# Projecting two value groups together, with 512 moving columns

## The chip, the cores and the metric

The kernel runs on one core of a Trainium2 chip. The metric is device time in microseconds, the median of several executions. Of each kernel one execution is also recorded by the hardware profiler; its times are counted from the first instruction. The core's engines are TensorE (PE, matmuls, with PEld for the loads of the stationary operand), VectorE (DVE), ScalarE (ACT), GpSimd (POOL) and SyncE (SP), whose queue issues nearly all DMA transfers. Each engine works through its own instructions in order and waits for others by semaphores.

## The reference

Two layers over a sequence of 512 tokens of width 1024. In each layer one projection of the residual stream feeds two mixers of eight heads of width 64 and an indexer:

```python
proj = jnp.einsum('bsd,dn->bsn', x, w_in)
qA, kA, vA, gA, qB, kB, vB, gB, qI, kI, wI = jnp.split(proj, SPLIT_POINTS, axis=-1)
oA = stick_breaking_attention(heads(qA, HEADS_A), heads(kA, HEADS_A), heads(vA, HEADS_A))
oB = dsa_sparse_attention(heads(qB, HEADS_B), heads(kB, HEADS_B), heads(vB, HEADS_B),
                          qI.reshape(b, s_len, IDX_HEADS, IDX_DIM), kI, wI, rel_bias, topk)
mix = jnp.concatenate([oA * jax.nn.silu(gA), oB * jax.nn.silu(gB)], axis=-1)
y = jnp.einsum('bsm,md->bsd', mix, w_out)
return layer_norm(ALPHA * x + y, ln_g, ln_b)
```

Mixer A is stick-breaking attention: with z the scaled scores, a key's weight is sigmoid(z) times the product of (1 - sigmoid(z)) over the keys between it and the query. Mixer B takes, for each query, the 128 keys that the indexer scores highest, and does a soft-max with a bias by relative position over them. The gate silu(g) is g times sigmoid(g).

## The kernel before

All products are made in three matmuls: each fp32 operand is split into a high part and a low rest (`hi`, `lo`), and high times high, low times high and high times low are summed in PSUM. The residual stream lies transposed in `XH` and `XL` as 4 token blocks by 8 chunks of 128 channels. `XN` holds it in its natural order; between the start of a layer and slot 59 that tile is free.

The projection is cut into units of 256 columns, named by group, half and kind: `("A", 1, "v")` is the values of the second four stick heads, `("B", 0, "v")` those of the first four soft-max heads. For queries, keys and gates (`project_t`, L274) the weights are stationary and 512 tokens move, one chunk of 128 columns after the other. For values (`project_v`, L286) the tokens are stationary and the 256 weight columns move, one token block after the other. Each unit's weights are two tiles of 1024 elements per partition. The class `Stream` loads them (two raw buffers, L193), splits them (ACT makes the high part, L212, POOL the low part, L215) into four buffers, and keeps about two tiles ahead (`prep_ahead`, at the end of each slot).

A layer is a loop over slots (L899), one attention task per slot: slots 0 to 23 are the indexer, 24 to 39 the four heads of A0, 40 to 55 those of A1, 56 to 71 those of B0, 72 to 87 those of B1; a task is one block of 128 queries of one head, with 128 to 512 keys. The order of all engines' work is written out by hand in this loop. Of a task, PE makes the scores in its slot (`product`, L518 and L523, into two PSUM buffers). A stick task then has a Sigmoid on ACT (L717), a scan on DVE a slot later (L722), and PE transposes the result three slots after the scores (L530). A soft-max task has a sum with the bias and a minimum on DVE (L762; the bias and mask are added on POOL a slot before, L753), an Exp on ACT (L767) and its transposes two slots after the scores. The transposed weights are copied by ACT (L727, L538) and their low parts made by DVE (L730, L541), and when a head is complete PE multiplies them with its values (L701) and the output is mixed: a copy on ACT (L600), a sum on DVE (L602) and, where the gate is there already, a product on POOL (L603). In some slots DVE stores bias plus mask of later heads in `XN` (L980).

The projection units fill PE between these steps. `fills` (L75) gives their order, each with a pin: the slot by which it is to be done. `fill` (L836) is called up to three times a slot and runs as many steps as the line between the pins asks for, counting 648 for three 512-wide matmuls and 324 for three 256-wide ones. What a unit leaves in PSUM is evacuated at the next `flush`, early in the following slot. The pins that matter:

```python
units += [("A", 1, "g"), ("A", 1, "k"), ("A", 1, "q"), ("A", 1, "v")]
units += [("A", 0, "g"), ("B", 0, "g"), ("B", 1, "g"), ("B", 0, "k"), ("B", 0, "q")]
units += [("B", 0, "v"), ("B", 1, "k"), ("B", 1, "q"), ("B", 1, "v")]
A_PINS = (29, 32.5, 36, 40, 44, 47.4, 50.6, 53.8, 56.8)
B_PINS = (62.5, 67, 71, 79)
```

So the values of A1 are made from slot 36 to 40 and those of B0 from 56.8 to 62.5; the gates are done by 29, 44, 47.4 and 50.6. A query chunk is evacuated by two ACT and two DVE instructions, a key chunk by the same and two DMA copies (`evac_q`, `evac_k`), a gate chunk by a Sigmoid on ACT and a product on DVE, and one more product on POOL if the head's output is there (`gate`, L582). B0's value blocks go from PSUM to their tile `vt` by ACT and DVE (`evac_v`, L355). A1's are first copied to `V_NOW`, in the tile `M`; three DMA copies shift them by one token into `V_PREV` (`shift_values`, L322), and two slots later DVE takes the difference and ACT and DVE split it (`value_steps`, L335). The tiles `vt` come from a pool of two.

Of the kernel before, what the change touches and what calls it, by code (L numbers as in the profile page):

```python
# [17 lines left out]
P = 128  # L18
# [39 lines left out]
A_PINS = (29, 32.5, 36, 40, 44, 47.4, 50.6, 53.8, 56.8)  # L58
# [12 lines left out]
HALF_SLOTS = 5  # L71
B_PINS = (62.5, 67, 71, 79)


def fills():  # L75

    units = [("I", 1, "q"), ("A", 0, "k"), ("A", 0, "q")]
    units += [("A", 1, "g"), ("A", 1, "k"), ("A", 1, "q"), ("A", 1, "v")]
    units += [("A", 0, "g"), ("B", 0, "g"), ("B", 1, "g"), ("B", 0, "k"), ("B", 0, "q")]
    units += [("B", 0, "v"), ("B", 1, "k"), ("B", 1, "q"), ("B", 1, "v")]  # L80
    return list(zip(units, HEAD_PINS + A_PINS + B_PINS, strict=True))


UNITS = [("A", 0, "v"), ("I", 0, "q")] + [u for u, _ in fills()]


# [16 lines left out]
def tile_hybrid(ctx: ExitStack, tc: tile.TileContext, xt, x, w_in, w_ki, w_out, ln_g, ln_b, rel_bias, onehot, out, depth=DEPTH):  # L103
# [69 lines left out]
    class Stream:  # L173
# [63 lines left out]
    units = [("A", 0, "v"), "ki", ("I", 0, "q")] + [u for u, _ in fills()]  # L237

    specs, index = [], {}
    for l in range(depth):  # L240
        for unit in units:
            index[l, unit] = len(specs)
            if unit == "ki":
                specs.append((w_ki[l], 8 * 72))
            else:
                specs += [(w_in[l, UNITS.index(unit), c], 1024) for c in range(2)]
        index[l, "o"] = len(specs)
        specs += [(w_out[l, half, mt], 1024) for half in range(2) for mt in range(4)]
# [27 lines left out]
    def project_t(l, unit, evac):  # L276
        for c in range(2):
            w = stream.get(index[l, unit] + c)
            acc = ppj.tile([P, S], F32, tag="pj", name="pj")
            for kc in range(KC):  # L280
                mm3(acc, [t[:, kc * P : (kc + 1) * P] for t in w], kc, kc == 0, kc == KC - 1, first_block(unit))
                if kc == KC - 1:
                    later.append(lambda c=c, acc=acc: evac(c, acc))
                yield cost(unit)

    def project_v(l, unit, vt, keys=None):  # L286
        i = index[l, unit]
# [8 lines left out]
        for tb in range(NTB):  # L296
# [4 lines left out]
            for kc in range(KC):  # L301
# [11 lines left out]
                if (tb, kc) == (NTB - 1, KC - 1) and unit[0] == "A":  # L313
                    later.append(shift_values)
                    pending.append([SHIFT_SLOTS[1], lambda: value_steps(vv)])
                yield 324 * n // W256


# [3 lines left out]
    def shift_values():  # L322
        V.memset(V_PREV[0:1, 0, :], 0.0)
        nc.sync.dma_start(V_PREV[1:113], V_NOW[0:112])
        nc.sync.dma_start(V_PREV[113:128], V_NOW[112:127])
        nc.sync.dma_start(V_PREV[0:1, 1:NTB], V_NOW[127:128, 0 : NTB - 1])

    def value_differences(engine, tbs=slice(0, NTB)):
        engine.tensor_tensor(V_PREV[:, tbs], V_PREV[:, tbs], V_NOW[:, tbs], ALU.subtract)
# [5 lines left out]
    def value_steps(vv):  # L335
        value_differences(V)
        for i in range(4):
            pending.append([i // 2, lambda i=i: value_part(vv, *divmod(i, 2))])

    def value_part(vv, low, half):  # L340
        t = slice(2 * half, 2 * half + 2)
# [46 lines left out]
    def first_units(keys, turn_keys, head_weights, evac_qi):  # L388
        unit = [index[0, u] for u in units[:3]]
# [13 lines left out]
        q_src = w_in[0, UNITS.index(units[2])].rearrange("c p n -> p c n")  # L403
# [154 lines left out]
    def layer(l):  # L558
# [23 lines left out]
        def gate(pair, p):  # L582
            assert pair < 4 or not pending
# [29 lines left out]
        def project(unit):  # L613
# [7 lines left out]
            QKV[unit] = [None, None]  # L621
            if c == "k":
                return project_t(l, unit, lambda j, p: evac_k(QKV[unit], j, p))
            return project_t(l, unit, lambda j, p: evac_q(QKV[unit], j, p, first_block(unit)))
# [192 lines left out]
        for unit, by in fills():  # L817
            total += 16 * cost(unit)
            queue.append(lambda unit=unit: project(unit))
            pins.append((by, total))  # L820
# [78 lines left out]
        for s in range(SLOTS + 3):  # L899
# [254 lines left out]
```

## Time and profile before

| | us |
|---|---|
| median of 3 runs (lowest, highest) | 633.32 (633.21, 633.35) |
| profiled execution | 633.23 |
| its span, first to last instruction | 631.4 |
| first layer's stick stage, slots 24 to 55 | 68.3 to 192.5 |
| first layer's soft-max stage, slots 56 to 87 | 192.5 to 274.7 (start of slot 87) |
| PE, DVE, ACT, POOL busy | 622.5, 494.7, 343.6, 366.4 |
| granted TensorE clock | 0.996 |

The stages' bounds are the starts of the first score matmul of the slot. In the profile a row of the order of time gives start, duration, engine, line, operation, what it writes and reads, the tile's shape and, in brackets, how long the engine was idle before and what ended that. A row of a group gives the count, then the busy time and mean ns, then idle time before. A matmul's duration includes its way through the array, so the pace of matmuls is the distance of their starts.

### The profile page before, as it was taken

The numbers are of one execution on the slowest core, as the hardware profiler recorded it, in microseconds if no ns is written. First come the engines' busy times: TensorE is split into PE (matmuls) and PEld (weight loads), VectorE is DVE, ScalarE is ACT, GpSimd is POOL, SyncE is SP. The second block draws the span as 40 slices with busy tenths as digits, with TensorE's granted clock in tenths as the row PEclk, the third lists the DMA queues.
The fourth block names the chain that finished last, engine by engine and source line by source line (L and its number), as shares of the span: only waits on it lengthen the run. The fifth ranks groups of instructions, "written<-read, shape, count | busy, mean of one in ns | idle before, by whom it ended". The sixth has DMA issues, their size and how long they took to land.

```text
span 631.4 us, 10261 instructions
## 1 busy us (share of the span) xinstructions
PE 622.5 (99%) x3501; PEld 542.7 (86%) x3501; DVE 494.7 (78%) x1058; ACT 343.6 (54%) x686; POOL 366.4 (58%) x380
## 2 busy tenths in 40 slices
PE   9999999999999999999999999999999999999995
PEld 7988888988889889878899888899888898898784
DVE  3878999999975775668845789999999667656676
ACT  5686545454447566883135855554535566678700
POOL 5563544468465776898134544525756577778721
PEclk9999999999999999999999999999999999999998
DMA  7624243222362475453314242323123725644402
GB/s 239 215 78 133 101 133 102 82 86 68 98 174 80 133 187 168 124 191 118 134 68 133 103 133 100 114 87 125 43 101 90 194 86 140 171 131 142 166 34 100
DMA packets 31779, 77.41 MB, mean 123 GB/s; under 512 B 6572, under 2 KB 10668, under 8 KB 31728
## 3 DMA queue, kind: packets, MB, share of 16 engines
q1 hardware_dynamic: 31440, 76.51, 39.1%
q8 instruction: 27, 0.44, 0.3%
q10 hardware_dynamic: 288, 0.26, 0.1%
q14 instruction: 24, 0.20, 0.1%
HBM read 61.84 MB, written 4.44 MB: 105 GB/s over the span
## 4 chain that ended last, share of the span: by engine, by line
PE 91%; ACT 3%; POOL 2%; DMA 1%; DVE 1%; issue 1%; DVEq 0%; SPq 0%; POOLq 0%; ACTq 0%
PE pj L266 15%; PE pj L268 15%; PE pj L267 15%; PE pjo L809 11%; PE o L701 5%; PE tr L530 5%; PE z L523 4%; PE pjv L303 4%; PE pjv L304 4%; PE pjv L305 4%; PE z L518 4%; PE pjv L428 2%; PE pjq L430 1%; POOL wlo L215 1%; ACT p L767 1%; ACT p L777 1%
## 5 line engine op out<-in xcount | busy, mean ns | idle before, releaser
L215 POOL TENSOR_TENSOR wlo<-raw,whi 128x256 fp32r<-128x256 f32 (+1 forms) x250 | 230.9, 954 | 142.1 <-ACT whi L212 141.2
L266 PE MATMUL pj<-XH,whi 128*128 128x512 f32 (+1 forms) x432 | 171.6, 397 | 0.0
L268 PE MATMUL pj<-XH,wlo 128*128 128x512 f32 (+1 forms) x432 | 166.4, 385 | 0.0
L267 PE MATMUL pj<-XL,whi 128*128 128x512 f32 (+1 forms) x432 | 166.1, 385 | 0.0
L268 PEld LDWEIGHTS pj<-XH,wlo 128*128 128x128 f32 x432 | 81.1, 188 | 16.1
L266 PEld LDWEIGHTS pj<-XH,whi 128*128 128x128 f32 x432 | 81.2, 188 | 13.1
L717 ACT ACTIVATE om<-z 128x128 f32<-128x128 f32 (+1 forms) x64 | 28.1, 438 | 118.1 <-issue 68.4
L267 PEld LDWEIGHTS pj<-XL,whi 128*128 128x128 f32 x432 | 81.4, 188 | 12.4
L212 ACT ACTIVATE whi<-raw 128x1024 fp32r<-128x1024 f32 x78 | 82.0, 1056 | 2.5 <-DMA raw<-in_w_in_dram 1.9
L722 DVE TENSOR_TENSOR_SCAN om<-om,future 128x128 f32<-128x128 f32 (+1 forms) x64 | 67.6, 1056 | 0.2
L603 POOL TENSOR_TENSOR M<-M,mixt 64x512 f32<-64x512 f32 x24 | 33.9, 1413 | 51.0 <-DVE mixt L602 36.0
L303 PE MATMUL pjv<-whi,XH 128*128 128x256 f32 x192 | 56.8, 296 | 0.0
L305 PE MATMUL pjv<-wlo,XH 128*128 128x256 f32 x192 | 54.3, 283 | 0.0
L304 PE MATMUL pjv<-whi,XL 128*128 128x256 f32 x192 | 54.2, 282 | 0.0
L854 DVE MAX8 m<-scores 128x8 f32<-128x256 f32 (+2 forms) x96 | 52.9, 551 | 0.1
L855 DVE MATCH_REPLACE8 scores<-m,scores 128x256 f32<-128x256 f32 (+2 forms) x96 | 52.1, 543 | 0.0
L767 ACT ACTIVATE p<-p,mn 128x128 f32<-128x128 f32 (+1 forms) x64 | 35.8, 560 | 23.9 <-DVE mn L762 23.5
L701 PE MATMUL o<-AT,vt 128*128 128x512 f32 (+7 forms) x256 | 48.6, 316 | 0.0
L809 PE MATMUL pjo<-whi,XH 128*128 128x512 f32 (+1 forms) x118 | 41.2, 387 | 0.0
L809 PE MATMUL pjo<-wlo,XH 128*128 128x512 f32 (+1 forms) x118 | 41.0, 383 | 0.0
L523 PE MATMUL z<-k,q 128*128 128x128 f32 (+3 forms) x128 | 40.9, 320 | 0.0
L541 DVE TENSOR_TENSOR AT<-tr,AT 128x128 fp32r<-128x128 f32 (+1 forms) x64 | 31.2, 488 | 11.7 <-ACT AT L538 11.3
(165 smaller groups left out, 1290.8 us busy)
## 6 DMA issues: line engine op xcount, KB each, us to landing
raw<-in_w_in_dram SPq DMA_DIRECT2D x66, 512.0 KB, 3.4
k<-k SPq DMA_DIRECT2D x32, 256.0 KB, 5.1
raw<-in_w_out_dram SPq DMA_DIRECT2D x14, 512.0 KB, 3.2
gbias<-f_dram SPq DMA_DIRECT2D x18, 256.0 KB, 3.9
XN<-in_x_dram SPq DMA_DIRECT2D x8, 256.0 KB
y_dram<-XN SPq DMA_DIRECT2D x4, 512.0 KB, 2.6
XN<-y_dram SPq DMA_DIRECT2D x8, 256.0 KB, 3.9
M<-M SPq DMA_DIRECT2D x4, 448.0 KB
```

The lines of the kernel that those rows point to most:

```text
L212: A.activation(hi, src, AF.Copy)
L215: low = lambda lo=lo[:, c], src=src[:, c], hi=hi[:, c]: lo_engine.tensor_tensor(lo, src, hi, ALU.subtract)
L266: T.matmul(o, w[0], XH[:, tb:, kc, :], start=first, stop=False)
L267: T.matmul(o, w[0], XL[:, tb:, kc, :], start=False, stop=False)
L268: T.matmul(o, w[1], XH[:, tb:, kc, :], start=False, stop=last)
L303: T.matmul(full, XH[:, tb, kc, :], whi, start=kc == 0, stop=False)
L304: T.matmul(full, XL[:, tb, kc, :], whi, start=False, stop=False)
L305: T.matmul(full, XH[:, tb, kc, :], wlo, start=False, stop=kc == KC - 1)
L523: T.matmul(self.z[:, :nn], c, d, start=False, stop=True)
L701: T.matmul(self.o[:m, sb * P :], vt[:, sb, self.hh * P : self.hh * P + m], at_block(self.at[j], sb, sb, NTB - sb), start=(sb, j) == (0, 0) ...
L722: V.tensor_tensor_scan(rev, rev, future[:, S - n :][:, ::-1], 1.0, ALU.mult, ALU.max)
L809: T.matmul(acc[:, cols], mixed[:, tb, m, :], w[:, cols], start=n == 0, stop=n == len(steps) - 1)
```

## The change

The units `("A", 1, "v")` and `("B", 0, "v")` become one unit, `PAIR`. Its four weight tiles each hold two chunks with 256 columns of the one and 256 of the other side by side, loaded by two transfers each. `project_pair` goes over the token blocks in two passes, two blocks in a pass with one PSUM buffer each. Its output is copied by ACT to the left half of `XN` (`staged`); A1's part is shifted and split from there as before, and B0's part stays until slots 46 and 48, when `split_staged` makes its high part on ACT and its low part on POOL. By then A0's tile of the value pool is free.

The pair stands where A1's values stood, pinned to slot 40. Only the first chunk of A1's keys and queries comes before it, the second chunk of each after it, by 42 and 44. The gates follow one place later: A0 by 47.4, B0 by 50.6, and B1 takes the place of the B0 values, from 56.8 to 62.5.

```diff
-A_PINS = (29, 32.5, 36, 40, 44, 47.4, 50.6, 53.8, 56.8)
+A_PINS = (29, 30.75, 32.5, 40, 42, 44, 47.4, 50.6, 53.8, 56.8)
...
+STAGED = (46, 48)
...
+PAIR = (("A", 1, "v"), ("B", 0, "v"))
...
+    units += [(("A", 1, "g"), both), (("A", 1, "k"), (0,)), (("A", 1, "q"), (0,)), (PAIR, None)]
+    units += [(("A", 1, "k"), (1,)), (("A", 1, "q"), (1,))]
+    units += [(u, both) for u in (("A", 0, "g"), ("B", 0, "g"), ("B", 0, "k"), ("B", 0, "q"))]
+    units += [(u, both) for u in (("B", 1, "g"), ("B", 1, "k"), ("B", 1, "q"), ("B", 1, "v"))]
...
-                    nc.sync.dma_start(raw[:, :n], src)
...
+                    if isinstance(src, list):
+                        for u, part in enumerate(src):
+                            nc.sync.dma_start(self.raw[i][:, u::2, :], part.rearrange("p (a b) -> p a b", b=W256))
+                    else:
+                        nc.sync.dma_start(raw[:, :n], src)
...
+    def project_pair(l, vt, staged):
+        i = index[l, PAIR]
+        vv = vt.rearrange("p t (h r) -> p t h r", r=P)
+        for tbs in ((0, 1), (2, 3)):
+            accs = {}
+            for j in range(4):
+                stream.prep(i + j)
+                stream.want = i + min(j + 2, 3) if tbs[0] == 0 else i + 3 + j
+                w = [t.rearrange("p (a b) -> p a b", b=S) for t in stream.done[i + j]]
+                for tb in tbs:
+                    if j == 0:
+                        if tb == NTB - 1:
+                            flush()
+                        accs[tb] = ppj.tile([P, S], F32, tag="pj", name="pjv")
+                    for m in range(2):
+                        kc = 2 * j + m
+                        T.matmul(accs[tb], XH[:, tb, kc, :], w[0][:, m], start=kc == 0, stop=False)
+                        T.matmul(accs[tb], XL[:, tb, kc, :], w[0][:, m], start=False, stop=False)
+                        T.matmul(accs[tb], XH[:, tb, kc, :], w[1][:, m], start=False, stop=kc == KC - 1)
+                        if kc == KC - 1:
+                            later.append(lambda tb=tb, acc=accs[tb]: A.activation(staged[:, tb], acc, AF.Copy))
+                            if tb == NTB - 1:
+                                now = staged[:, :, :W256]
+                                later.append(lambda: shift_values(now))
+                                pending.append([SHIFT_SLOTS[1], lambda: value_steps(vv, now)])
+                        yield 648
...
         def gate(pair, p):
-            assert pair < 4 or not pending
+            assert pair < 4 or turn["steps"] == 4
...
+        def split_staged(half):
+            if not half:
+                QKV[PAIR[1]] = vp.tile([P, NTB, 4 * P], F32R, tag="v", name="vt")
+            t = slice(2 * half, 2 * half + 2)
+            vv = QKV[PAIR[1]].rearrange("p t (h r) -> p t h r", r=P)[:, t]
+            src = XN[:, t, W256:S].rearrange("p t (h d) -> p t h d", d=HD)
+            A.activation(vv[:, :, :, :HD], src, AF.Copy)
+            for i in range(2):
+                G.tensor_tensor(vv[:, i, :, HD:], src[:, i], vv[:, i, :, :HD], ALU.subtract)
...
+            total += 32 * 648 if unit == PAIR else 8 * len(cs) * cost(unit)
...
+            if s in STAGED:
+                split_staged(STAGED.index(s))
```

More of the change, by code (lines that the diff above doesn't have):

```diff
@@ L71, with all_units @@
 HALF_SLOTS = 5
+STAGED = (46, 48)
 B_PINS = (62.5, 67, 71, 79)
+PAIR = (("A", 1, "v"), ("B", 0, "v"))
 def fills():
[L77 to L84, printed above, removed]
+    both = (0, 1)
+    units = [(("I", 1, "q"), both), (("A", 0, "k"), both), (("A", 0, "q"), both)]
+    units += [(("A", 1, "g"), both), (("A", 1, "k"), (0,)), (("A", 1, "q"), (0,)), (PAIR, None)]
+    units += [(("A", 1, "k"), (1,)), (("A", 1, "q"), (1,))]
+    units += [(u, both) for u in (("A", 0, "g"), ("B", 0, "g"), ("B", 0, "k"), ("B", 0, "q"))]
+    units += [(u, both) for u in (("B", 1, "g"), ("B", 1, "k"), ("B", 1, "q"), ("B", 1, "v"))]
+    return [(u, cs, by) for (u, cs), by in zip(units, HEAD_PINS + A_PINS + B_PINS, strict=True)]
+def all_units():
+    units = [("A", 0, "v"), ("I", 0, "q")]
+    for u, cs, _ in fills():
+        units += [v for v in (PAIR if u == PAIR else (u,)) if v not in units]
+    return units
+UNITS = all_units()
 def unit_col(u):
@@ L274, in cost, with project_t @@
         return 648 * (NTB - first_block(unit)) // NTB
-    def project_t(l, unit, evac):
-        for c in range(2):
-            w = stream.get(index[l, unit] + c)
+    def project_t(l, unit, evac, cs=(0, 1)):
+        for c in cs:
+            w = stream.get(index[l, unit, c])
             acc = ppj.tile([P, S], F32, tag="pj", name="pj")
@@ L286, in project_v @@
     def project_v(l, unit, vt, keys=None):
-        i = index[l, unit]
+        i = index[l, unit, 0]
         if keys is None:
@@ L314, in project_v @@
                     later.append(shift_values)
-                    pending.append([SHIFT_SLOTS[1], lambda: value_steps(vv)])
+                    pending.append([SHIFT_SLOTS[1], lambda: value_steps(vv, V_NOW)])
                 yield 324 * n // W256
+    def project_pair(l, vt, staged):
[3 more added lines that the diff above has]
+            accs = {}
+            for j in range(4):
+                stream.prep(i + j)
[18 more added lines that the diff above has]
+                        yield 648
@@ L319, in tile_hybrid, with shift_values @@
     V_NOW, V_PREV = (M[:, i : i + 2, :].rearrange("p x (y d) -> p (x y) d", d=W256) for i in (6, 4))
     pending = []
-    def shift_values():
+    def shift_values(now=V_NOW):
+        turn["steps"] = 0
         V.memset(V_PREV[0:1, 0, :], 0.0)
[L324 to L329, printed above, removed]
+        nc.sync.dma_start(V_PREV[1:113], now[0:112])
+        nc.sync.dma_start(V_PREV[113:128], now[112:127])
+        nc.sync.dma_start(V_PREV[0:1, 1:NTB], now[127:128, 0 : NTB - 1])
@@ L331, in value_parts, with value_differences @@
+    def value_differences(engine, now=V_NOW):
+        engine.tensor_tensor(V_PREV, V_PREV, now, ALU.subtract)
     def value_parts(vv):
@@ L333, in value_parts, with value_steps @@
             value_part(vv, *divmod(i, 2))
-    def value_steps(vv):
-        value_differences(V)
+    def value_steps(vv, now):
+        value_differences(V, now)
         for i in range(4):
@@ L388, in first_units @@
     def first_units(keys, turn_keys, head_weights, evac_qi):
-        unit = [index[0, u] for u in units[:3]]
+        unit = [index[0, ("A", 0, "v"), 0], index[0, "ki"], index[0, ("I", 0, "q"), 0]]
         q_raw = vp.tile([P, NTB, 4 * P], F32, tag="v", name="q_raw").rearrange("p (c a) b -> p c (a b)", c=2)
@@ L611, in mix_split, with project @@
             split(hi, lo, src, lo_engine=lo_engine)
-        def project(unit):
+        def project(unit, cs=(0, 1)):
+            if unit == PAIR:
+                QKV[PAIR[0]] = vp.tile([P, NTB, 4 * P], F32R, tag="v", name="vt")
+                return project_pair(l, QKV[PAIR[0]], XN[:, :, :S])
             kind, i, c = unit
@@ L816, in layer @@
         pins = [(0, PREFILL * 648)]
-        for unit, by in fills():
-            total += 16 * cost(unit)
-            queue.append(lambda unit=unit: project(unit))
+        for unit, cs, by in fills():
+            total += 32 * 648 if unit == PAIR else 8 * len(cs) * cost(unit)
+            queue.append(lambda unit=unit, cs=cs: project(unit, cs))
             pins.append((by, total))
```

23 lines of the change are left out of this document (15 added, 8 removed).

## The prediction

> **What bounds the kernel now.** I read the page first (busy shares and the chain that ended last), then busy time by stretch, the matrix engine's order of time for its pace, and the other engines' order of time where the change puts work.
>
> ```profile
> span 631.4 us, 10261 instructions
> ...
> PE 622.5 (99%) x3501; PEld 542.7 (86%) x3501; DVE 494.7 (78%) x1058; ACT 343.6 (54%) x686; POOL 366.4 (58%) x380
> ...
> PE 91%; ACT 3%; POOL 2%; DMA 1%; DVE 1%; issue 1%; DVEq 0%; SPq 0%; POOLq 0%; ACTq 0%
> ```
>
> TensorE (PE) is busy 99% of the span and carries 91% of the chain, so whatever shortens its instruction stream shortens the kernel, and whatever makes it wait lengthens it. The profiled execution took 633.23 us with a span of 631.4; the median of the runs is 633.32, 0.09 above, so sums made against the profiled execution carry over.
>
> The two stretches that the change touches, by engine:
>
> ```profile
> 126.30:141.50 15.20, 15.20 (x79) 12.78 (x78) 14.37 (x29) 7.81 (x15) 9.28 (x9) 1.00 0.28 89
> ...
> 205.00:218.00 13.00, 13.00 (x82) 11.51 (x81) 10.42 (x22) 5.74 (x15) 10.12 (x9) 1.00 0.48 133
> ```
>
> The columns after the length are PE, weight load, VectorE (DVE), ScalarE (ACT) and GpSimd (POOL). PE has no gap in either. In the stick stage (first row) DVE is at 14.37 of 15.20. In the soft-max stage (second row) ACT has 7 of 13 us free, DVE 2.6.
>
> **The matmuls: what is gained.** The two value units of a layer are 2 x 4 blocks x 8 chunks x 3 = 192 matmuls of 256 moving columns; the pair does the same in 96 of 512. The pace, from the first and the 23rd matmul of an unbroken run of 256-wide ones, and from a run of 90 that are 512 wide in the chain:
>
> ```profile
> L303 PE MATMUL pjv<-whi,XH 128*128 128x256 f32 x192 | 56.8, 296 | 0.0
> ```
>
> ```profile
> 108.51 0.28 PE L304 MATMUL pjv<-whi,XL 128*128 128x256 f32 x1
> ...
> 111.14 0.28 PE L305 MATMUL pjv<-wlo,XH 128*128 128x256 f32 x1
> ```
>
> ```profile
> 281.99 20.41 PE pjo L809 x90
> ```
>
> 2.63 us / 22 = 119.5 ns against 20.41 / 90 = 226.8 ns. Two narrow ones less a wide one are 239.0 - 226.8 = 12 to 13 ns; the 192 of each of the three lines fall to 64 narrow and 64 wide, so 3 x 64 = 192 pairs in both layers: **-2.4 us**, or 0.6 us in each layer at the pair (slots 32 to 40) and 0.6 where the old B0 values stood (slots 57 to 62), now taken by the gate of B1. The pace is a property of the width, not of waiting; nothing hides it. On this the Trainium skill ("TensorE: Matmul & The Clock Gate", Back-to-back issue gap) speaks against the change: it gives a gap of N/2.4 + 2.5 ns at full clock, by which a pair would save 2.5 ns and the kernel an estimated 0.5 us. The measured paces leave some 13 ns over N/2.4 for both widths, so the rows decide.
>
> **The weights of the pair.** Four tiles come as eight transfers instead of four, in shorter pieces, and the first pass over the pair uses a tile per slot instead of one per two. The split of a tile is one ACT instruction and four on POOL:
>
> ```profile
> L212 ACT ACTIVATE whi<-raw 128x1024 fp32r<-128x1024 f32 x78 | 82.0, 1056 | 2.5 <-DMA raw<-in_w_in_dram 1.9
> ...
> L215 POOL TENSOR_TENSOR wlo<-raw,whi 128x256 fp32r<-128x256 f32 x192 | 155.9, 845 | 113.7 <-ACT whi L212 113.2
> ```
>
> 1.06 + 4 x 0.85 = 4.4 us per tile. By the loop's order the third and fourth tile are issued about 1.4 slots before their use, that is 5.3 us (the first stretch above is four slots of 3.8), and most of POOL's idle time before such pieces is a wait for ACT, not the other way round. ACT waited 1.9 us for raw weights in the whole span. I take 0; if that cover is gone, a tile late by its whole split holds PE 4.4 us, at most twice a layer. SP's queue gets four more issues a layer, ahead of the shift of the values, which is due two slots later: 0 again, and at most the same. The low parts of the B0 values move from DVE (slots 57 to 62) to POOL, four pieces of about 0.85 us at slots 46 and 48, and their evacuation from eight narrow ACT copies to four wide ones with two more at those slots; ACT is at 7.81 of 15.20 and POOL at 9.28 in the first stretch above, and nothing reads these values before slot 62: 0. The gates of A0 and B0 move by one place within the stick stage, with the same ACT and DVE work each: 0.
>
> **VectorE's peak in the stick stage.** In slots 41 to 44 the evacuations of the second key and query chunk (two DVE instructions each) replace two gate products (one each):
>
> ```profile
> 131.74 0.69 DVE L587 TENSOR_TENSOR sig<-pj,sig 128x512 f32<-128x512 f32 x1 [0.63 <-ACT sig L585]
> ...
> 145.06 1.75 DVE L722 TENSOR_TENSOR_SCAN om<-om,future 128x512 f32<-128x512 f32 x1
> ```
>
> ```profile
> 149.81 0.60 PE L530 MATMUL tr<-ident,om 128*128 128x128 f32 x4
> ```
>
> ```profile
> 221.79 0.69 DVE L376 TENSOR_TENSOR k<-pj,k 64x512 fp32r<-64x512 f32 x1
> ```
>
> DVE is latest at the scan that ends at 146.81, 3.0 us before PE transposes its result. It gets 2 x 0.69 = 1.4 us more by then, and PE comes 0.6 earlier; 1.0 us is left. I take 0, with 0 to 1 us a layer for the range.
>
> **The gates: what it costs.** Every gate starts with a Sigmoid on ACT. Before, all gates fall in the stick stage, whose own function is Sigmoid. The unit B1 gate now lies between slots 56.8 and 62.5, inside the soft-max stage, whose function is Exp. A change of function has a price:
>
> ```profile
> L717 ACT ACT_TABLE_LOAD x2 | 2.6, 1283 | 0.0
> L767 ACT ACT_TABLE_LOAD x2 | 2.6, 1283 | 0.8 <-DVE mn L762 0.8
> ```
>
> ```profile
> 131.12 0.59 ACT L585 ACTIVATE sig<-pj 128x512 f32<-128x512 f32 x1
> ```
>
> ```profile
> 194.14 1.28 ACT L767 ACT_TABLE_LOAD   x1 [0.41 <-DVE mn L762]
> 195.44 0.40 ACT L767 ACTIVATE p<-p,mn 128x128 f32<-128x128 f32 x1
> ```
>
> One load for Sigmoid and one for Exp in each layer now. Each of the two gate chunks will need both, so eight loads more, and the load for Exp comes only after the wait for DVE's row minimum (0.41 us idle, then the load). The chunks end where half and all of the old B0 values end, since the work per slot is the same; their evacuations at 201.79 and 212.26 mark the places. Here is ACT around them, then DVE:
>
> ```profile
> 201.79 0.36 ACT L358 ACTIVATE vt<-pjv 128x256 fp32r<-128x256 f32 x1
> 202.49 0.39 ACT L538 ACTIVATE AT<-tr 128x256 fp32r<-128x256 f32 x1 [0.34 <-PE tr L530]
> 204.00 0.72 ACT L767 ACTIVATE p<-p,mn 128x512 f32<-128x512 f32 x1 [1.12 <-DVE mn L762]
> ...
> 204.84 0.59 ACT L600 ACTIVATE mixt<-o 64x512 f32<-64x512 f32 x1
> ...
> 210.80 0.51 ACT L767 ACTIVATE p<-p,mn 128x256 f32<-128x256 f32 x1 [0.34 <-DVE mn L762]
> ...
> 212.26 0.36 ACT L358 ACTIVATE vt<-pjv 128x256 fp32r<-128x256 f32 x1
> 212.52 0.27 ACT L538 ACTIVATE AT<-tr 128x128 fp32r<-128x128 f32 x1
> 212.68 0.61 ACT L767 ACTIVATE p<-p,mn 128x384 f32<-128x384 f32 x1
> ...
> 214.13 0.60 ACT L600 ACTIVATE mixt<-o 64x512 f32<-64x512 f32 x1 [0.75 <-PE o L701]
> ...
> 218.91 1.05 ACT L212 ACTIVATE whi<-raw 128x1024 fp32r<-128x1024 f32 x1
> ```
>
> ```profile
> 205.46 0.69 DVE L602 TENSOR_TENSOR mixt<-o,mixt 64x512 f32<-64x512 f32 x1 [0.89 <-ACT mixt L600]
> ...
> 212.65 0.42 DVE L359 TENSOR_TENSOR vt<-pjv,vt 128x256 fp32r<-128x256 f32 x1 [0.54 <-ACT vt L358]
> ...
> 214.76 0.68 DVE L602 TENSOR_TENSOR mixt<-o,mixt 64x512 f32<-64x512 f32 x1 [1.48 <-ACT mixt L600]
> ...
> 217.42 0.67 DVE L762 CUSTOM_DVE_ANT_0 p<-z,p 128x512 f32<-128x512 f32 x1
> ```
>
> First chunk, in the times of before: 201.79 + 1.28 + 0.59 = 203.66; the copy, 204.05; the second load, 205.33; the exponential and its sum take 0.84 as before, so the copy for the head's mix starts at 206.17, not 204.84: **1.3 us late**. The 1.5 us that ACT waited there are used up. DVE stands behind this copy, in order, at 205.46, and its next idle time is at 212.65, so all between, with the minimum for which the exponential at 210.80 waits, is 1.3 late. Second chunk: 212.26 + 1.3 = 213.56; load and Sigmoid, 215.43; copy, 215.70; load, 216.98; exponential and sum 0.70; the copy for the mix starts at 217.68, not 214.13: **3.55 us late**, and with it DVE's 214.76 and the minimum at 217.42, which ends at 221.6.
>
> PE's places that wait for this, and POOL between them:
>
> ```profile
> 220.61 0.28 PE L518 MATMUL z<-k,q 128*128 128x256 f32 x1
> ...
> 225.91 0.87 PE L701 MATMUL o<-AT,vt 128*128 128x512 f32 x4
> ```
>
> ```profile
> 220.04 2.56 POOL L215 TENSOR_TENSOR wlo<-raw,whi 128x512 fp32r<-128x512 f32 x2 [0.83 <-ACT whi L212]
> 222.54 2.72 POOL L753 TENSOR_TENSOR p<-gbias,mask 128x256 f32<-128x256 f32 x3
> ```
>
> ```profile
> 223.62 0.69 DVE L541 TENSOR_TENSOR AT<-tr,AT 128x512 fp32r<-128x512 f32 x1
> ```
>
> The scores have two buffers; those at 220.61 go where the minimum of 217.42 read. PE, by now early by the 0.6 us of its wide matmuls at this place, wants them at 220.0 and gets them at 221.6: 1.0 us later than before. The weights' split at 218.91, POOL's low parts and its bias sums at 222.54 are 3.55 late, so are the next minimum and the low parts at 223.62, which then end at 227.9. The values at 225.91 need them; PE is at 226.9 by then and stops for 1.0 more. So PE leaves this place 2.0 us late, against a layer whose earlier part is 0.6 early: +1.4 us a layer. From both sides: no stall at all (0, that is -1.2 a layer), or the whole 3.55 (+2.9 a layer).
>
> **Sum.** 633.23 + 2 x (2.0 - 0.6) = 636.0, and 0.09 for the median: **636.1 us**. Its own range is 634.7 to 638.5.
>
> **Rivals.** *All hidden (faster).* ACT is free more than half the time in the soft-max stage, and PE transposes an exponential two slots after it is made; if the tables are loaded in that slack, or the head's mix doesn't hold DVE, only the -2.4 remains: 630.9. It decides if the minimum of 217.42 comes less than 2.5 us late (its end, 218.1, to PE's 220.61). Against it: the two notes of DVE idle behind ACT's copy, 0.89 and 1.48, show that the copy already sets DVE's pace. *Half hidden (no change).* If the first chunk's 1.3 us is absorbed, the second alone makes the mix 2.2 late; the minimum ends at 220.3, about when PE wants it, and the values stop for 0.9, together some +0.6 against -0.6: 633.3. *VectorE's peak decides too.* If it loses another microsecond in the stick stage beyond the 1.0 left, the two layers add 2: 638. *A dearer switch.* If each change of function held ACT for twice the load, two more times 1.28 per chunk, with no idle time left, add 5.1 a layer: 646. The exponential at 195.44 begins 1.30 after the load began, which leaves no room for it. The Trainium skill ("ScalarE: Activation LUTs", What ACT_TABLE_LOAD costs) has this rule: about 1283 ns for the load and about 1380 ns for a drain, some 2.66 us a switch; the trace agrees on the load and shows no drain. *That the change doesn't do what it says* would show as loads without stalls, which is the first rival.
>
> **Chances.** Forecast 0.57, all hidden 0.21, half hidden 0.13, VectorE's peak 0.06, dearer switch 0.03. With 0.2% (1.3 us) as what a measurement can tell from no change: faster 0.22 (with the near side of half hidden), same 0.15 (the rest of half hidden, and the lower edge of the forecast), slower 0.63. The range must reach to the fastest rival, 0.21 being too much to leave out: 630.7 to 638.6.
>
> **What would show it.** 13 table loads instead of 5, eight of them between the exponentials of the B0 heads; PE idle, or a wider step, of about 1 us before the scores and the values at the first soft heads' end, in both layers; matmuls of the pair at 227 ns; no idle time of PE in slots 32 to 45. The prediction is wrong if PE's row stays without gaps in the B0 stage, or if the pair itself, or the transposes near slot 46, show waits.

## The result and the profile after

| | before | after |
|---|---|---|
| median of 4 runs each (lowest, highest), us | 633.34 (633.21, 633.78) | 640.12 (639.85, 640.42) |
| profiled execution, us | 633.23 | 640.33 |
| ratio, 95% interval | | 1.0106 (1.0088 to 1.0123) |

The changed kernel is slower by 6.8 us. The forecast was 636.1, so the direction is right, the size is not, and 640.1 lies 1.5 us above the end of the range. The page of the kernel after, the lines that answer to the first ones of before:

```profile
span 638.5 us, 9898 instructions
...
PE 623.4 (98%) x3309; PEld 531.9 (83%) x3309; DVE 491.8 (77%) x1050; ACT 356.3 (56%) x690; POOL 365.0 (57%) x388
...
PE 81%; ACT 6%; DVE 4%; POOL 4%; issue 3%; DMA 1%; SPq 0%; DVEq 0%; ACTq 0%; POOLq 0%
```

192 matmuls are gone, as planned, but the chain that ended last now runs through ACT, DVE and POOL for 14% of the span where it was 6%: PE is waiting for them. ACT is busy 12.7 us longer. The next view says where. It is busy time by stretch of the first layer; the stretches are slots 32 to 39, 56 to 61 and 62 to 67, from the start of one slot's scores to that of another. First before, then after:

```profile
95.62:126.31 30.69, 30.69 (x204) 28.01 (x203) 29.13 (x63) 15.90 (x32) 12.72 (x17) 1.00 0.31 94
...
192.51:210.84 18.33, 18.33 (x147) 17.74 (x145) 13.20 (x33) 12.03 (x28) 13.16 (x12) 1.00 0.24 74
210.84:231.90 21.06, 21.06 (x108) 17.46 (x107) 16.07 (x35) 12.68 (x29) 15.01 (x12) 1.00 0.65 162
```

```profile
96.02:126.18 30.16, 30.16 (x156) 25.49 (x154) 26.00 (x58) 14.58 (x28) 15.42 (x19) 1.00 0.23 74
...
192.61:211.49 18.88, 17.90 (x98) 14.81 (x96) 11.24 (x26) 13.55 (x24) 12.48 (x14) 1.00 0.34 104
211.49:234.92 23.43, 21.93 (x107) 17.26 (x108) 16.34 (x37) 16.34 (x33) 13.93 (x13) 1.00 0.52 134
```

The pair's stretch is shorter by 0.53 us and PE is busy in all of it: this is the gain of the wide matmuls. The other two are longer by 0.55 and 2.37, and PE is idle in them for 0.98 and 1.50. The account of the 7.10 us by which the profiled executions differ, from the starts of the slots' first scores in both (each number is how much more the changed kernel needs for that stretch; slot 55 goes with the slots behind it, since the next unit begins in it and its last three projection matmuls are 512 wide now, and were 256 wide):

| | first layer | second layer |
|---|---|---|
| slots 32 to 39 (pair) | -0.53 | -0.53 |
| slots 40 to 54 (rest of the stick stage) | -0.09 | -0.09 |
| slots 55 to 67, and no more to 78 | +3.25 | +3.76 |
| slots 79 to 84 | +0.45 | +0.74 |

That makes 6.96. Another 0.40 arises in the first 5 us of the program, where the kernels don't differ in what they do (0.0 to 0.5 in most of the runs below, 1.8 in one), and at the ends of the layers the changed kernel gets 0.26 back. All of the loss is in the soft-max stage, and nearly all in the first half of it, where the gate of B1 now is. PE's idle times there, from its order of time after (in brackets how long PE waited, and for what):

```profile
199.09 0.33 PE L583 MATMUL tr<-ident,p 128*128 128x128 f32 x1 [0.27 <-DVE AT L796]
...
211.49 0.44 PE L571 MATMUL z<-k,q 128*128 128x384 f32 x1 [0.72 <-DVE mn L828]
...
222.91 0.38 PE L571 MATMUL z<-k,q 128*128 128x256 f32 x1 [1.21 <-DVE mn L828]
...
227.98 0.30 PE L583 MATMUL tr<-ident,p 128*128 128x128 f32 x1 [0.29 <-DVE AT L594]
```

Before, PE had no such entry in this stretch. The last two, at the scores of slot 65 and ahead of slot 67, are the two stops of the forecast. The first two, ahead of slot 59 and at slot 62, were not in it. (In the starts of the slots a stop is 0.2 to 0.45 more than in the bracket, since the profile models the ends of matmuls; the four come to 3.7 us.) The groups of ACT, after:

```profile
L833 ACT ACT_TABLE_LOAD x6 | 7.7, 1283 | 0.1
L638 ACT ACT_TABLE_LOAD x4 | 5.1, 1283 | 0.1
L783 ACT ACT_TABLE_LOAD x2 | 2.6, 1283 | 0.0
...
L179 ACT ACT_TABLE_LOAD x1 | 1.3, 1283 | 1.2 <-PEq L1211 1.2
```

```profile
L229 ACT ACTIVATE whi<-raw 128x1024 fp32r<-128x1024 f32 x78 | 81.9, 1055 | 6.1 <-DMA raw<-in_w_in_dram 5.6
```

13 loads, eight more than before, as forecast. The last row is new: ACT waited 5.6 us for raw weights, where it was 1.9. ACT's order of time in the stretch, after:

```profile
192.53 1.06 ACT L229 ACTIVATE whi<-raw 128x1024 fp32r<-128x1024 f32 x1 [1.47 <-DMA raw<-in_w_in_dram]
193.50 0.57 ACT L418 ACTIVATE q<-pj 64x512 fp32r<-64x512 f32 x1
...
195.10 1.28 ACT L833 ACT_TABLE_LOAD   x1
...
202.84 1.28 ACT L638 ACT_TABLE_LOAD   x1
...
205.02 1.28 ACT L833 ACT_TABLE_LOAD   x1
...
207.16 0.59 ACT L653 ACTIVATE mixt<-o 64x512 f32<-64x512 f32 x1
...
218.78 0.60 ACT L653 ACTIVATE mixt<-o 64x512 f32<-64x512 f32 x1
```

The mix copies start at 207.16 and 218.78; before they started at 204.84 and 214.13. That is 2.3 and 4.65 us late against 1.3 and 3.55 in the forecast: both are about a microsecond later than the tables explain. The microsecond is there before the first gate: the query evacuation of slot 55's end is at 193.50, not 192.12, and the load for the Exp at 195.10, not 194.14, because ACT first sat 1.47 us, in order, at the split of a weight tile that hadn't landed. Before, this split came at 198.21, behind the exponential of slot 57 and with no wait:

```profile
192.12 0.59 ACT L365 ACTIVATE q<-pj 64x512 fp32r<-64x512 f32 x1 [0.84 <-PE pj L268]
...
198.21 1.04 ACT L212 ACTIVATE whi<-raw 128x1024 fp32r<-128x1024 f32 x1
```

The code says why it moved. `project_t` calls `stream.get`, which asks for tiles up to two ahead when a chunk begins; `project_v`, which stood in this place, raises what it asks for only when its second token block begins. So ACT now comes to the split of the tile behind the unit's own at 191.06, 7.1 us sooner than before (198.21). And the tile is late because its raw buffer comes free late. SP's queue issues its load, before and then after:

```profile
185.23 0.34 SPq L193 DMA_DIRECT2D raw<-in_w_in_dram  x1
```

```profile
188.06 0.34 SPq L211 DMA_DIRECT2D raw<-in_w_in_dram  x1
```

2.8 us later; ACT's wait ends 4.5 us behind that, when the tile is there. What holds the buffer is POOL, which makes the low parts of the tile that was in it. Before and then after:

```profile
181.98 3.22 POOL L215 TENSOR_TENSOR wlo<-raw,whi 128x256 fp32r<-128x256 f32 x4
```

```profile
184.06 6.76 POOL L232 TENSOR_TENSOR wlo<-raw,whi 128x256 fp32r<-128x256 f32 x8
```

POOL comes to them 2.1 us later, behind the product of a head's mix that waits for VectorE (it starts at 182.60 and not at 180.50); the buffer is free after four of them, 3.22 us on before and 3.98 after.

VectorE is late in its turn: the sum of that mix starts at 181.76 and not at 179.67. From slot 41 on it works nearly without a break, so what is added there stays. First come the evacuations of the second key and query chunk, the 1.4 us that the forecast counted: the scan of slot 43's task starts at 146.84 and not at 145.06 (0.4 of it from the program's start). Then the scan of slot 49's task takes longer; it and the sum of the mix, before and then after:

```profile
166.59 3.77 DVE L722 TENSOR_TENSOR_SCAN om<-om,future 128x256 f32<-128x256 f32 x1
...
179.67 0.69 DVE L602 TENSOR_TENSOR mixt<-o,mixt 64x512 f32<-64x512 f32 x1
```

```profile
167.73 5.29 DVE L788 TENSOR_TENSOR_SCAN om<-om,future 128x256 f32<-128x256 f32 x1
...
181.76 0.69 DVE L655 TENSOR_TENSOR mixt<-o,mixt 64x512 f32<-64x512 f32 x1
```

All other scans of this size take at most 1.23 us in both kernels. While this one runs, POOL makes low parts of weights without a gap, in the changed kernel with the two pieces of `split_staged` among them (1.42 us at 168.96). That the scan is longer because of those two fits the rows; no run separates it.

### The profile page after: what moved, and what is told of

Its sections match the earlier page's. It is cut to its first block, busy times and chain, and to the rows that moved or that the text cites. A ratio compares the mean times of both kernels' runs of the same rounds, so it can differ in the third digit from the quotient of the medians.

```text
span 638.5 us, 9898 instructions
## 1 busy us (share of the span) xinstructions
PE 623.4 (98%) x3309; PEld 531.9 (83%) x3309; DVE 491.8 (77%) x1050; ACT 356.3 (56%) x690; POOL 365.0 (57%) x388
## 4 chain that ended last, share of the span: by engine, by line
PE 81%; ACT 6%; DVE 4%; POOL 4%; issue 3%; DMA 1%; SPq 0%; DVEq 0%; ACTq 0%; POOLq 0%
PE pjo L875 13%; PE pj L290 13%; PE pj L292 13%; PE pj L291 13%; PE o L767 5%; PE tr L583 4%; PE z L576 4%; PE z L571 3%; PE pjv L361 2%; PE pjv L359 2%; PE pjv L360 2%; PE pjv L481 2%; POOL wlo L232 2%; DVE XN L1046 2%; ACT p L833 2%
## 5 line engine op out<-in xcount | busy, mean ns | idle before, releaser
L290 PEld LDWEIGHTS pj<-XH,whi 128*128 128x128 f32 x432 | 81.5, 189 | 12.7
L788 DVE TENSOR_TENSOR_SCAN om<-om,future 128x128 f32<-128x128 f32 (+1 forms) x64 | 68.9, 1076 | 0.2
L656 POOL TENSOR_TENSOR M<-M,mixt 64x512 f32<-64x512 f32 x22 | 31.2, 1419 | 50.0 <-DVE mixt L655 38.8
L571 PE MATMUL z<-k,q 128*128 128x128 f32 (+3 forms) x128 | 39.7, 311 | 3.8 <-DVE mn L828 3.8
L576 PE MATMUL z<-k,q 128*128 128x128 f32 (+3 forms) x128 | 40.9, 320 | 0.0
L875 PE MATMUL pjo<-whi,XL 128*128 128x512 f32 (+1 forms) x118 | 39.5, 381 | 0.0
L796 DVE SCALAR_TENSOR_TENSOR AT<-tr,AT 128x128 fp32r<-128x128 f32 (+1 forms) x64 | 30.6, 478 | 8.3 <-ACT AT L793 7.8
```

Of the source, the lines that this page charges most:

```text
L290: T.matmul(o, w[0], XH[:, tb:, kc, :], start=first, stop=False)
L571: T.matmul(self.z[:, :nn], a, b, start=True, stop=False)
L576: T.matmul(self.z[:, :nn], c, d, start=False, stop=True)
L788: V.tensor_tensor_scan(rev, rev, future[:, S - n :][:, ::-1], 1.0, ALU.mult, ALU.max)
L875: T.matmul(acc[:, cols], mixed[:, tb, m, :], w[:, cols], start=n == 0, stop=n == len(steps) - 1)
```

## The experiments

The theory at this point: the wide matmuls gain what was forecast; the loss has two causes, the table loads of the moved gate (by the forecast's chain, some 2.6 us a layer against no loads at all) and the early tile request. The rivals: that the pair itself, or VectorE in the stick stage, costs; that a table load costs by the piece and not by a chain; that ACT merely has too much to do. "Before" was run on the same chip with each group: 633.73 us in the first (first four kernels), 633.55 in the second (next four), 633.45 in the last.

| | median us | ratio to before (95%) |
|---|---|---|
| Copy for Sigmoid | 633.12 | 0.9997 (0.9981 to 1.0013) |
| late request | 637.87 | 1.0059 (1.0044 to 1.0074) |
| both | 631.54 | 0.9962 (0.9947 to 0.9977) |
| before, with gate and values exchanged | 640.32 | 1.0103 (1.0086 to 1.0120) |
| Sigmoid in the first chunk only | 632.48 | 0.9986 (0.9977 to 0.9995) |
| Sigmoid in the second chunk only | 634.64 | 1.0019 (1.0010 to 1.0029) |
| Tanh, with an instruction more | 634.08 | 1.0008 (0.9999 to 1.0017) |
| all gates in the stick stage | 647.47 | 1.0215 (1.0201 to 1.0229) |
| Tanh, without one | 631.24 | 0.9964 (0.9950 to 0.9978) |

**No other function.** The gate's Sigmoid of B1 becomes a Copy, which needs no table; the sigmoid of the last four heads is left out.

```diff
-            A.activation(s, p, AF.Sigmoid)
+            A.activation(s, p, AF.Copy if pair >= 6 else AF.Sigmoid)
```

> The changed kernel with a plain copy in place of the Sigmoid in the gate of B1 alone (the other gates keep theirs): the gate's sigmoid is left out of the last four heads, all instructions and waits stay, the eight extra table loads go. Theory 1 (the table loads make ACT, then DVE late, and PE stops for the scores and values of the first soft heads): 5 table loads; the stops at slots 60 to 67 go; what is left is the 1.5 to 2.0 us for which ACT now waits for a raw weight tile at slot 55, worth 0.4 to 1.0 us a layer; 631.5 to 633. Theory 2 (that wait for the weight tile, a slot and a half earlier in the stream than before, is the cause, and the loads lie in idle time): about 639 to 640, unchanged.

633.12 us: 7.0 less than the changed kernel, and five loads. The raw wait stays (5.7 us), and with it the stop ahead of slot 59 (0.25 us in the first layer and 1.4 in the second, by the slots' starts).

**The request later.** The gate's first chunk asks one tile ahead when it begins, and for the second tile when it is half done.

```diff
-            w = stream.get(index[l, unit, c])
+            late = unit == ("B", 1, "g") and c == 0
+            w = stream.get(index[l, unit, c], 1 if late else 2)
...
+                if late and kc == KC // 2:
+                    stream.want = index[l, unit, c] + 2
```

> The changed kernel, but the first chunk of B1's gate asks for weights one tile ahead instead of two until its fifth step, so that the third tile is split where it was split before the change. Theory 1 alone: the tables stay, so the late chain of the prediction stays, 636 to 637; ACT's wait for the raw tile before slot 56 is gone. Theory 2 alone: 630.9, the gain of the wide matmuls.

637.87 us, 2.3 less than after and 0.9 above the 636 to 637 expected for the loads alone. VectorE and POOL are as late here as in the changed kernel (POOL's product of the mix starts at 182.66), so with POOL late it is the time of the request that decides whether ACT waits. This kernel has the eight loads and not the early tile, that is, just what the forecast summed up, and its ACT and PE can be held against that sum:

```profile
197.89 1.04 ACT L229 ACTIVATE whi<-raw 128x1024 fp32r<-128x1024 f32 x1
...
201.58 1.28 ACT L641 ACT_TABLE_LOAD   x1
...
205.90 0.59 ACT L656 ACTIVATE mixt<-o 64x512 f32<-64x512 f32 x1
...
217.53 0.59 ACT L656 ACTIVATE mixt<-o 64x512 f32<-64x512 f32 x1
```

```profile
221.66 0.39 PE L574 MATMUL z<-k,q 128*128 128x256 f32 x1 [1.27 <-DVE mn L831]
...
226.73 0.30 PE L586 MATMUL tr<-ident,p 128*128 128x128 f32 x1 [0.33 <-DVE AT L597]
```

The split is back at 197.89 without a wait. The mix copies start at 205.90 and 217.53, where the working gave 206.17 and 217.68; the scores of slot 65 start at 221.66, where it gave 221.6. From slot 55 to 78 the kernel loses 2.10 and 2.11 us in the two layers; the forecast has 2.0. Another 0.36 and 0.65 come at slots 79 to 84, for which it has nothing. The difference to the changed kernel from slot 55 to 78, 1.15 and 1.65 us, is the price of the early tile.

**Both.** The two edits together.

> The copy in place of B1's Sigmoid and the later request for the tile together. If these two are all that went wrong: 630.9 (633.3 less the 2.4 of the wide matmuls), PE without stops in the B0 stage. Anything above 631.5 would mean a third cause, in the pair or in the moved gates.

631.54 us, 2.2 less than before. (It is at the bound of 631.5 that was set for a third cause, but the kernel before was 0.4 slower in this group than at the result, so the gain falls 0.2 short of the 2.4 expected.) PE has no stop in slots 56 to 67, and each of the four stretches in which 96 matmuls became 48 is shorter by 0.53: -2.1 in all. This is what the pair is worth when nothing spoils it. The loads are then 637.87 - 631.54 = 6.3 us; ACT's other instructions are as many here as with the Sigmoid, so it isn't merely that ACT has too much to do. The early tile alone, without the loads, is 633.12 - 631.54 = 1.6 (the runs behind the first number spread from 632.0 to 637.1); with the loads it is 2.3. The pair's own evacuations, transfers and shorter pieces cost nothing that can be seen while the request is late.

**The exchange without the pair.** The kernel before, with the gate of B1 and the values of B0 in each other's place in the order of units.

```diff
-    units += [("A", 0, "g"), ("B", 0, "g"), ("B", 1, "g"), ("B", 0, "k"), ("B", 0, "q")]
-    units += [("B", 0, "v"), ("B", 1, "k"), ("B", 1, "q"), ("B", 1, "v")]
+    units += [("A", 0, "g"), ("B", 0, "g"), ("B", 0, "v"), ("B", 0, "k"), ("B", 0, "q")]
+    units += [("B", 1, "g"), ("B", 1, "k"), ("B", 1, "q"), ("B", 1, "v")]
```

> The kernel before, in which only the unit B1 gate and the unit B0 values change places: the values are made by slot 50.6, the gate between 56.8 and 62.5; no pair, all values 256 wide. If the place of the gate (table loads and the early tile) is the whole loss: 640.1 + 2.4 = 642.5. If the pair has a cost of its own, less than 642; if the moved key and query chunks do, less too.

640.32 us: moving the gate is enough to lose 6.6 us. But it isn't the same sum as in the changed kernel. The request is early here too, yet the tile has landed:

```profile
192.16 1.05 ACT L212 ACTIVATE whi<-raw 128x1024 fp32r<-128x1024 f32 x1
```

There is no bracket: SP issued the load at 186.03, and ACT's raw wait in the whole span is 2.2 us. So the early request alone doesn't make the late tile; it takes the late POOL of the changed kernel as well, and that is why I expected too much here. POOL isn't late here because VectorE isn't: the sum of the mix starts at 180.48, although the slots there are 1.0 us later than before. From slot 55 to 78 this kernel loses 2.3 us a layer, the loads again. The rest is 0.6 a layer in slots 46 to 50 and 0.4 at slot 81. The 0.6 is no stop: PE has no gap there, and it is what the 256-wide values of B0 take more than the 512-wide gate that they replace.

**One chunk at a time.** Late request, and a Sigmoid in only one of the gate's two chunks, the first and then the second (`pair == 6` for the second kernel); the other chunk's sigmoid is left out.

```diff
-            A.activation(s, p, AF.Sigmoid)
+            A.activation(s, p, AF.Copy if pair == 7 else AF.Sigmoid)
```

> The kernel with the later request (x2), with the Sigmoid in the first chunk of B1's gate only; the second chunk's sigmoid is left out (a copy in its place). Two extra loads a layer, in slot 59. Theory of a chain (the first chunk's delay alone lies under the 2.5 us that the minimum of slot 63 has to spare, and is only carried to the second): 631.5 to 632, as with no Sigmoid at all. Theory of a price per load (each of the eight loads costs its 1.28 us, 6.3 us for all by x2 less x3): half of it, 634.7.

> The same with the Sigmoid in the second chunk only (slot 62); the first chunk's sigmoid is left out. Chain: the mix is 2.2 us late instead of 3.55, PE stops little for the scores and about 0.9 for the values of slot 66, 0.6 to 1.0 a layer: 632.5 to 633.5; the two halves then don't add up to x2. Price per load: 634.7.

Four loads in the first chunk cost 632.48 - 631.54 = 0.9 us, four in the second 634.64 - 631.54 = 3.1, all eight 6.3, more than the sum. In the first of the two kernels PE loses 0.5 us a layer at slots 62 and 63 and nothing at 65: ACT's slack takes up the rest. In the second:

```profile
220.16 0.39 PE L574 MATMUL z<-k,q 128*128 128x256 f32 x1 [0.38 <-DVE mn L831]
...
225.23 0.30 PE L586 MATMUL tr<-ident,p 128*128 128x128 f32 x1 [0.31 <-DVE AT L597]
```

By the starts of the slots these are 0.64 and 0.61, 1.25 a layer, where the forecast's "half hidden" has 0.3 and 0.9; another 0.4 and 0.7 come at slots 79 to 82, which it doesn't have and which bring the kernel 1.1 us above the range expected. A price by the piece would have put both kernels at the same time; that rival is out. The lateness of the first chunk is handed on to the second, which is the forecast's chain.

**All gates in the stick stage.** If the function is the trouble, the gate of B1 can stay where Sigmoid is loaded, and another unit fill slots 57 to 62.

```diff
-A_PINS = (29, 30.75, 32.5, 40, 42, 44, 47.4, 50.6, 53.8, 56.8)
+A_PINS = (29, 30.75, 32.5, 40, 42, 44, 46.6, 49.1, 51.7, 54.2, 56.8)
...
-B_PINS = (62.5, 67, 71, 79)
+B_PINS = (64, 71, 79)
...
-    units += [(u, both) for u in (("A", 0, "g"), ("B", 0, "g"), ("B", 0, "k"), ("B", 0, "q"))]
-    units += [(u, both) for u in (("B", 1, "g"), ("B", 1, "k"), ("B", 1, "q"), ("B", 1, "v"))]
+    units += [(u, both) for u in (("A", 0, "g"), ("B", 0, "g"), ("B", 1, "g"), ("B", 0, "k"), ("B", 0, "q"))]
+    units += [(u, both) for u in (("B", 1, "k"), ("B", 1, "q"), ("B", 1, "v"))]
```

> The changed kernel with all three gates between slots 44 and 52 (five units by slot 56.8 instead of four) and three units instead of four from there to slot 79; Sigmoid stays, no gate among the exponentials. If the place among the exponentials is the cause: 5 loads and near 631. Against it: PE has less to fill the soft-max slots with, and POOL gets ten weight tiles instead of eight in those slots; if that binds, 632 to 635 with stops of another kind.

647.47 us, and five loads. The stick stage takes 9.9 us more than before in the first layer for the unit that is added, and the soft-max stage should give them back, with one unit less. By slot 70 it has given back 3.6. With less to fill in, PE is ahead of the other engines and stops, first ahead of slot 60:

```profile
213.64 0.44 PE L583 MATMUL tr<-ident,p 128*128 128x128 f32 x2 [2.21 <-DVE AT L796]
```

```profile
212.41 0.56 DVE L828 CUSTOM_DVE_ANT_0 p<-z,p 128x384 f32<-128x384 f32 x1 [3.44 <-POOL p L819]
```

```profile
214.40:217.80 3.40, 3.40 (x11) 2.74 (x10) 2.02 (x4) 3.10 (x7) 0.79 (x1) 0.51 0.30 80
```

PE waits for a low part that DVE makes behind a minimum, and the minimum waited 3.44 us for POOL's sum of bias and mask, which POOL came to at 211.46, behind two pieces of a weight tile (208.97 to 211.51). That is the rival of the expectation, POOL with more weights to split in these slots, though far beyond its 632 to 635. The brackets of PE from slot 56 to 69 add up to 4.4 us. The last row is a stretch behind the first stop: its last number but two is the granted clock, 0.51, and 512-wide matmuls start 0.43 us apart there and not 0.23. The same happens in the second layer, and in the attention slots of no other kernel. So the filling work isn't only load; it also gives the other engines the time for theirs, and the place that the values of B0 left had to be filled with something.

**A function that needs no load.** sigmoid(x) is half of one plus tanh(x/2). The Trainium skill ("ScalarE: Activation LUTs", Table sets: the hidden batching unit) lists tanh in the same set as exp. Late request, and:

```diff
-            A.activation(s, p, AF.Sigmoid)
+            if pair >= 6:
+                A.activation(s, p, AF.Tanh, scale=0.5)
+                V.tensor_scalar(s, s, 0.5, 0.5, ALU.mult, ALU.add)
+            else:
+                A.activation(s, p, AF.Sigmoid)
```

> The later request, and the sigmoid of B1's gate computed as 0.5 + 0.5 tanh(p / 2): Tanh shares its table with Exp in this build (five loads in the program), the halving and the sum are one more DVE instruction per chunk, at most 0.7 us, four in all. If loads are the cause and not the gate's place: as x3, 631.5, at most 0.5 more, faster than the kernel before by 1.5 to 2.4 us. If the gate's other work there (DVE products, POOL) costs something: 633 or more.

Five loads: the trace agrees with the Trainium skill. But 634.08 us, 2.5 more than with Copy. VectorE in this kernel, then the same place with Copy and the late request, then PE's stop:

```profile
203.50 2.52 DVE L643 TENSOR_SCALAR sig<-sig 128x512 f32<-128x512 f32 x1
206.05 0.69 DVE L654 TENSOR_TENSOR M<-pj,sig 128x512 f32<-128x512 f32 x1
```

```profile
203.52 0.69 DVE L650 TENSOR_TENSOR M<-pj,sig 128x512 f32<-128x512 f32 x1
```

```profile
210.82 0.44 PE L574 MATMUL z<-k,q 128*128 128x384 f32 x1 [0.65 <-DVE mn L835]
```

The added instruction takes 2.52 us (1.14 in the second chunk) where its neighbours of the same size take 0.69, and the minimum behind it is late. POOL shows what it met:

```profile
202.82 2.53 POOL L232 TENSOR_TENSOR wlo<-raw,whi 128x512 fp32r<-128x512 f32 x2
205.32 0.42 POOL L826 TENSOR_TENSOR p<-gbias,mask 128x128 f32<-128x128 f32 x1
```

POOL works without a gap from 202.82 to 205.74, and the vector instruction ends at 206.02. The Trainium skill ("SBUF — State Buffer", Who interferes with whom) says that VectorE and GpSimd share a pair of SBUF ports, that a `tensor_scalar` from SBUF to SBUF may take it, and that who comes second waits for the whole instruction of the other. That fits the row; no run here separates it from other causes.

**The same without an instruction more.** "One plus" goes into the vector product that makes the gate, and the half into the two instructions that add a head's two halves of the values (`mix`).

```diff
+            if pair >= 6:
+                A.activation(s, p, AF.Tanh, scale=0.5)
+                V.scalar_tensor_tensor(M[:, pair, :], s, 1.0, p, op0=ALU.add, op1=ALU.mult)
+                made.add(("g", pair))
+                return
             A.activation(s, p, AF.Sigmoid)
...
-            A.activation(t[hi], o[lo], AF.Copy)
+            half = 0.5 if pair >= 6 else 1.0
+            A.activation(t[hi], o[lo], AF.Copy, scale=half)
             if ("g", pair) in made:
-                V.tensor_tensor(t[hi], o[hi], t[hi], ALU.add)
+                if pair >= 6:
+                    V.scalar_tensor_tensor(t[hi], o[hi], half, t[hi], op0=ALU.mult, op1=ALU.add)
+                else:
+                    V.tensor_tensor(t[hi], o[hi], t[hi], ALU.add)
```

> The whole result is computed, with 5 loads, the later request of the gate's first chunk, and no instruction added: the sigmoid of both chunks is half of one plus tanh of half the argument, the "one plus" is in the vector product that forms the gate, and the half is in the two instructions that add the halves of the values (the scale of the copy, and a factor in the sum on VectorE). In the tanh run before this one the product was preceded by an instruction of its own that took 2.52 us on VectorE in the first chunk (beside POOL's tensor work, 1.14 us in the second), and the block maximum behind it came 2 us late at the next soft head, which is where TensorE stopped. Chain theory (a table load is late, an instruction that takes its place is not): the same as with Copy and the late request, 631.5 (631.2 to 631.9), no stop of TensorE in slots 56 to 67, faster than before by 1.8 to 2.2 us. Rival (the tanh itself or its scale costs, or what the tanh run showed came from the tanh and not from the added vector instruction): a stop of 0.4 to 0.6 us at slots 62 and 63 in both layers as in that run, 633.0 to 634.0.

```profile
span 629.3 us, 9886 instructions
...
PE 620.1 (99%) x3309; PEld 532.2 (85%) x3309; DVE 491.7 (78%) x1050; ACT 345.2 (55%) x682; POOL 364.4 (58%) x384
```

```profile
L643 DVE SCALAR_TENSOR_TENSOR M<-sig,pj 128x512 f32<-128x512 f32 x4 | 2.7, 686 | 2.2 <-ACT sig L642 2.2
...
L795 ACT ACT_TABLE_LOAD x2 | 2.6, 1283 | 0.0
L845 ACT ACT_TABLE_LOAD x2 | 2.6, 1283 | 0.2
```

631.24 us, 2.2 less than before and 8.9 less than the change as it was made, and nothing is left out. PE doesn't stop in slots 56 to 67 of either layer. The product, which now reads one operand from SBUF and one from PSUM, takes 686 ns; so the tanh was not what cost in the run before, its extra instruction was.

## Why the prediction was right and wrong

1. *The wide matmuls, -2.4 us.* Right: four stretches of -0.53, 2.1 in all, and 2.2 by the medians. The matmuls go at 227 ns, and PE doesn't stop at the pair. By the gap that the Trainium skill gives for an isolated matmul ("TensorE: Matmul & The Clock Gate", Back-to-back issue gap) it would have been an estimated 0.5; the rows of before were the better guide.
2. *The weights, "I take 0".* Here the forecast failed. The step looked at the pair's own tiles, and for those 0 is right. It gave the gate the place of the values without asking when a gate asks for its weights. `project_t` brings ACT to the tile behind the unit 7.1 us before `project_v` did; VectorE and behind it POOL are 2.1 us late, so the raw buffer and with it SP's transfer are late; and ACT, in order, stands 1.47 us at the split with the query evacuations and the Exp behind it. That costs 1.15 and 1.65 us a layer, 2.8 in the profiled executions and 2.3 by the medians of the changed kernel and of the one with the late request. The step even named the way to see it, ACT's wait for raw weights (1.9 us before, 5.6 after), but bounded it for the wrong place. It also put the low parts of the B0 values on POOL at 0 because nothing reads them before slot 62; they stand beside the scan that takes 5.29 us and not 3.77, though that they lengthen it is not shown. The fallback, "at most twice a layer 4.4", was too wide to be of use and did not go into the range.
3. *VectorE's peak, 0.* Right for PE: no stop in slots 41 to 55. But the step asked only whether the transposes come in time. VectorE's lateness doesn't go away: 1.4 us at the scan of slot 43 as counted, more with the scan of slot 49, 2.1 at the sum of the head's mix. It is what makes POOL late, and so a link of the late tile of point 2.
4. *The gates, +2.0 a layer at the soft-max heads.* Right, as the kernel with the late request shows: +2.1, with ACT's times to 0.3 us and the scores of slot 65 to 0.1. The division was a little off: the first chunk already costs 0.5 at slots 62 and 63, where the forecast had it absorbed by waits, and the second place stops PE for 0.6 at the transposes and not 1.0 at the values. That the sum agrees to 0.1 is in part luck, since these two errors cancel. With the 0.53 that the wide matmuls gain in the same slots, the loads cost 2.63 a layer in these slots; the forecast has 2.6.
5. *Left out.* 0.45 and 0.74 us at slots 79 to 84. A few tenths are there in most of the kernels with the loads, and 0.3 in the second layer of the two best. At that place ACT's split of the mixed output waits longer for a product on POOL than before. What makes that late was not settled.

*All hidden* is what the kernel would do without the loads and the early tile: 630.9 forecast, 631.24 and 631.54 measured. *Half hidden* is what one chunk with a Sigmoid does. *A dearer switch* is out: the Exp starts 1.30 us after its load in all kernels. The Trainium skill ("ScalarE: Activation LUTs", What ACT_TABLE_LOAD costs) is right on 1283 ns for the load, and again no drain shows. The sum, made good: 633.23 - 2.1 (matmuls) - 0.2 (slots 40 to 54) + 5.3 (loads, slots 55 to 67) + 2.8 (tile) + 1.2 (slots 79 to 84) + 0.1 (the program's start and the layers' ends) = 640.3. Of the 4.3 us that the forecast's 636.0 lacks, 2.8 are the tile and 1.2 the slots 79 to 84.

## What to carry to other kernels

When a unit of work takes another's place, compare what the two ask for and when, not only how long they take: the order of requests to a shared queue and an in-order engine moves with the code, even if the matmuls stay where they were. An engine whose lateness stops nothing in its own stage, as VectorE's here, can still make the next stage's weights late. A function from another table set, put in a stage that has its own, costs by what waits behind it, and not by 1.28 us a load: two loads in the first chunk cost a layer 0.5 us, two more in the second 1.6, and all four together 3.2. Before moving such work back, look for the same function within the stage's own table, and put the arithmetic that it needs into instructions that are there already.

## What the runs showed of the hardware

A VectorE instruction from SBUF to SBUF took 2.52 us in the first chunk and 1.14 in the second, in both layers, where a product of the same size with one operand in PSUM takes 0.69 beside the same work on POOL. Tanh and Exp alternate on ScalarE without a load (five loads in the program, as before). After a stop of TensorE of 2.2 us in the kernel with all gates in the stick stage, the granted clock was 0.51 for 3.4 us; stops of up to 1.27 us in the other kernels left it at 1.00. And taking filling work out of a stage in which TensorE is never idle (slots 56 to 67 of the kernel before) didn't shorten it in proportion: of 9.9 us added to the stick stage, 3.6 came back by slot 70.
